# Two more kinds of traffic in the first FFN: ten pairs as seven block products, and weight blocks split ahead along another route

## The chip, the cores and the metric

The kernel runs on one core of a Trainium2 chip. The metric is device time in microseconds (us) of one execution, lower is better. The kernel before takes 1269.9 us, the median of 3 runs (1269.84 to 1270.08).

A core has engines that run side by side, each through its own queue of instructions in order: TensorE (PE in the profile, with PEld for the loads of its weights), VectorE (DVE), ScalarE (ACT), GpSimd (POOL) and SyncE (SP). SP, and here also POOL, issue transfers (DMAs); an instruction that waits holds up all that stands behind it in its own queue and nothing else, until somebody needs its result.

## The reference

Two layers over 512 tokens with 16 learned tokens in front (528 columns), width 1024. Each layer is a mixer and an FFN:

```
def mixer_sublayer(h, ...):
    u = rms_norm(h, pre_g);  z = u @ w_in       # q,k,v, forget logits, conv and short-conv inputs
    y = concat[ FoX attention (8 heads), Conformer conv module, short gated conv ]
    y = head_rms_norm(y) @ w_out
    return h + rms_norm(y, post_g)

def ffn_sublayer(h, pre_g, post_g, w_up, conv_w, w_down):
    u = rms_norm(h, pre_g)
    z = causal_depthwise_conv(u @ w_up, conv_w)  # w_up: 1024 x 5632, 3 taps
    g, up = jnp.split(z, 2, axis=-1)             # 2816 columns each
    y = (silu(g) * up) @ w_down                  # 2816 x 1024
    return h + rms_norm(y, post_g)
```

All inputs and outputs are float32.

## The kernel before, in words

**Splitting.** Every product is made in TensorE's fp32r form out of two rounded parts of each operand: `hi` is the rounded value, `lo` is what is left, and a product is the sum of hi·hi, hi·lo and lo·hi, three matmuls for each block of 128 rows of the contraction (`mm3`, L833, and `product`, L2281). Each weight block of 512 KB is therefore loaded raw by a DMA, rounded to `hi` by ACT ("CAST") and `lo` is made by DVE (raw minus hi). `prep_one` does this some blocks ahead of TensorE; the kernel calls the tiles `raw`, `whi`/`wlo`, `shi`/`slo`.

**The FFN.** The 2816 gate columns and the 2816 up columns make 22 *pairs* f of 128 gate and 128 up columns. They run in three parts, f = 0 to 7, 8 to 14 and 15 to 21; after each part come eight *down* products (one for each 128 output rows, over that part's pairs). A plain pair is 2 blocks x 8 row groups x 3 matmuls x 2 column halves = 96 matmuls of 264 columns. Between TensorE's products ACT evacuates them and DVE and ACT do the three-tap convolution, the gate, and the split of the result (`ffn_gate`; its rounded part is `ghi`, the rest `glo`).

**Seven block products.** A pair in the set `SEVEN[l]` is computed by `seven_pair` as a 2x2 block matrix product with seven instead of eight block products (Winograd's form of Strassen's method): 7 x 4 row groups x 3 = 84 matmuls of 264 columns. In place of the up block it needs sums of weight blocks: a block `c`, a summed block `b` (tiles `shi`, `slo`, one buffer each) and a half block `d` (a free `y` pair). The sums of the input columns are made once per layer (`t`).

**Where the weight sums come from.** They are made beforehand and kept in DRAM (`w_sum`), in one of two ways. `sum_steps` makes them by accumulating DMAs of GpSimd: three copies on SP and three accumulations on POOL for each pair; either spread over a mixer, whose order of work a planner with due times sets, or in the FFN, one step at each pair, started by a small copy on POOL ("tick", L2199). `down_sums` makes them with DVE during the down products: two loads, four additions and two stores for each pair. For this it uses four spare slices of the residual tile `h` (`spare_tile(0)` to `spare_tile(3)`, 1024 columns each). The residual is kept in DRAM from the end of the first part until the last seven pair (`h_dram`), so these slices are free in the second and third part; `raw_tile` also uses them for raw weight blocks, two of seven from slices 2 and 3.

**Blocks split ahead.** Six 512 KB blocks of the next layer's `w_in` are split in the first FFN and stored as hi and lo (`w_split`), so that the next mixer only has to load them. `store_one` runs at each pair of the second part (f = 8 to 14): it splits the block that the last call fetched, with tiles `shi`/`slo` of the seven pairs, and stores both parts on GpSimd's queue, then fetches the next one on SP into a raw tile.

**What sets the order.** In the FFN it is the order of the written loops, with a few constraints (`tc.issue_after`), which order two instructions of the same engine without a wait between engines. A scheduler fills the queues from there; a load waits for the last reader or writer of its target buffer.

## Time and profile before

| | |
|---|---|
| median of 3 runs | 1269.9 us (1269.84 to 1270.08) |
| profiled execution: own time, span | 1270.68 us, 1269.0 us |
| PE busy | 1249.8 us (98%), 9590 instructions |
| PEld busy | 1198.2 us (94%) |
| DVE busy | 920.9 us (73%) |
| ACT busy | 705.2 us (56%) |
| POOL busy | 162.0 us (13%) |
| first FFN: first gate convolution; first down product evacuated; first seven pair | at 285.1; 365.3; 524.2 us |
| second FFN: last product of a seven pair; last gate convolution | at 1205.4; 1217.3 us |

The span is the time from the first to the last instruction of the profiled execution; its own time as measured is 1.7 us more. A row of the *chain of waits* follows the work that ended last. A row of a *timeline* is one instruction: start, duration, engine, line, operation, output, input, and in brackets how long its engine sat idle before it and what ended that. A row of *windows* gives for each stretch (from:to, length) the busy time and number of instructions of PE, PEld, DVE, ACT and POOL, then the granted clock of TensorE, the busy share of the DMA engines and their rate in GB/s. SPq and POOLq are the queues from which SP and POOL issue transfers; "DMA to landing" is the time from an issue to the transfer's end.

### The profile page before, as it was taken

What the parts mean: (1) busy time and instruction counts of PE and PEld (TensorE: products, weight loads), DVE (VectorE), ACT (ScalarE), POOL (GpSimd) and SP (SyncE); (2) the same over time, 40 slices, a digit from 0 to 9 for tenths busy, and PEclk for the clock granted to TensorE, in tenths of its full rate; (3) what the DMA queues carried; (4) which work ended last, traced back from release to release, by engine and by line L of the source; (5) the groups of instructions that cost most, each with busy time, mean ns of one, the idle gap of its engine ahead of it and who ended that gap; (6) DMA issues with size and microseconds to landing.
All of it is one profiled execution on the core that took longest, in us unless ns stands there. A gap on an engine that the chain in (4) does not pass through costs nothing.

```text
span 1269.0 us, 24272 instructions
## 1 busy us (share of the span) xinstructions
PE 1249.8 (98%) x9590; PEld 1198.2 (94%) x9590; DVE 920.9 (73%) x1569; ACT 705.2 (56%) x1365; POOL 162.0 (13%) x343
## 2 busy tenths in 40 slices
PE   8999999999999999999999999999999999999997
PEld 8998898999999999999999988999999799979996
DVE  7887866589874665587688878656799748756954
ACT  7254576654444643476673545775554447526763
POOL 1324311001101100000003244110021000000000
PEclk9999999999999999999999999999999999999999
DMA  7257231726558634544552584547166655475611
GB/s 243 81 155 175 72 102 53 249 86 151 182 164 313 212 112 142 205 165 144 192 205 61 159 191 113 143 118 233 70 166 184 172 176 169 152 241 160 202 61 67
DMA packets 76146, 197.93 MB, mean 156 GB/s; under 512 B 8240, under 2 KB 18608, under 8 KB 75520
## 3 DMA queue, kind: packets, MB, share of 16 engines
q1 hardware_dynamic: 64048, 162.69, 40.0%
q0 software_dynamic: 11984, 33.69, 11.1%
q8 instruction: 75, 1.23, 0.4%
q14 instruction: 39, 0.32, 0.1%
HBM read 162.17 MB, written 44.30 MB: 163 GB/s over the span
## 4 chain that ended last, share of the span: by engine, by line
PE 66%; DVE 2%; ACT 1%; issue 0%; DMA 0%; POOL 0%; DVEq 0%; ACTq 0%
PE psum L833 45%; PE psum L2281 14%; PE psum L1403 2%; PE psum L1667 2%; PE psum L970 1%; PE psum L1633 1%; PE psum L1589 0%; DMA h<-w_sum 0%; DVE yp L1046 0%; PE psum L1733 0%; PE psum L1319 0%; DVE h L1056 0%; POOL dm L1604 0%; DVE ulo L1064 0%; DVE wlo L649 0%
## 5 line engine op out<-in xcount | busy, mean ns | idle before, releaser
L833 PE MATMUL psum<-y,whi 128*128 128x264 f32 (+3 forms) x1968 | 384.7, 299 | 2.7 <-ACT yp L2403 1.4
L833 PEld LDWEIGHTS psum<-y,whi 128*128 128x128 f32 x1968 | 305.1, 188 | 17.2 <-ACT yp L2403 2.6
L833 PE MATMUL psum<-uhi,whi 128*128 128x264 f32 (+1 forms) x1264 | 310.3, 288 | 1.6 <-ACT uhi L2065 0.8
L833 PE MATMUL psum<-ulo,whi 128*128 128x264 f32 (+1 forms) x1264 | 304.1, 284 | 0.6 <-DVE ulo L2067 0.4
L833 PE MATMUL psum<-uhi,wlo 128*128 128x264 f32 (+1 forms) x1264 | 303.2, 284 | 0.0
L833 PE MATMUL psum<-y,wlo 128*128 128x264 f32 (+3 forms) x984 | 273.9, 297 | 1.1 <-DVE wlo L789 1.1
L833 PEld LDWEIGHTS psum<-uhi,whi 128*128 128x128 f32 x1264 | 216.0, 188 | 5.9 <-issue 1.6
L833 PEld LDWEIGHTS psum<-ulo,whi 128*128 128x128 f32 x1264 | 216.1, 188 | 1.3 <-DVE ulo L2067 0.6
L833 PEld LDWEIGHTS psum<-uhi,wlo 128*128 128x128 f32 x1264 | 215.6, 188 | 0.0
L833 PEld LDWEIGHTS psum<-y,wlo 128*128 128x128 f32 x984 | 177.6, 188 | 6.7 <-DVE wlo L789 1.6
L2169 DVE SCALAR_TENSOR_TENSOR c<-zs,pv,c 128x528 f32<-128x528 f32 (+1 forms) x176 | 130.9, 757 | 18.4 <-ACT c L2167 16.4
L648 ACT CAST whi<-raw 128x1024 fp32r<-128x1024 f32 (+1 forms) x67 | 68.2, 1021 | 98.4 <-PE psum L833 72.6
L789 DVE TENSOR_TENSOR wlo<-raw,whi 128x1024 fp32r<-128x1024 f32 (+2 forms) x80 | 95.4, 1203 | 29.8 <-ACT whi L785 29.5
L649 DVE TENSOR_TENSOR wlo<-raw,whi 128x1024 fp32r<-128x1024 f32 (+1 forms) x67 | 79.4, 1185 | 28.1 <-ACT whi L648 28.0
L785 ACT CAST whi<-raw 128x1024 fp32r<-128x1024 f32 (+2 forms) x80 | 81.7, 1031 | 24.9 <-PE psum L833 18.0
L1149 DVE SCALAR_TENSOR_TENSOR cacc<-apad,pv,cacc 128x528 f32<-128x528 f32 x120 | 87.7, 772 | 0.1
L2167 ACT ACTIVATE c<-zs,pv 128x528 f32<-128x528 f32 (+1 forms) x88 | 63.1, 727 | 7.0 <-DVE zs L2132 2.7
L2281 PE MATMUL psum<-uhi,whi 128*128 128x258 f32 (+1 forms) x216 | 61.2, 284 | 0.0
L2281 PE MATMUL psum<-ulo,whi 128*128 128x258 f32 (+1 forms) x216 | 61.0, 283 | 0.0
L2281 PE MATMUL psum<-uhi,wlo 128*128 128x258 f32 (+1 forms) x216 | 60.5, 282 | 0.0
L2281 PE MATMUL psum<-t,shi 128*128 128x258 f32 (+1 forms) x288 | 54.2, 283 | 0.0
L1667 PE MATMUL psum<-pf,vals 128*128 128x400 f32 (+3 forms) x160 | 50.7, 399 | 0.6 <-POOL pf L1647 0.6
(273 smaller groups left out, 2193.2 us busy)
## 6 DMA issues: line engine op xcount, KB each, us to landing
raw<-in_w_dram SPq DMA_DIRECT2D x115, 512.0 KB, 4.5
h<-in_w_dram SPq DMA_DIRECT2D x27, 512.0 KB, 4.8
raw<-in_w_dram SPq DMA_DIRECT2D x30, 448.0 KB, 5.1
raw<-w_sum SPq DMA_DIRECT2D x18, 512.0 KB, 5.1
h<-w_sum SPq DMA_DIRECT2D x18, 512.0 KB, 5.4
h<-in_w_dram POOLq DMA_DIRECT2D x16, 512.0 KB, 3.8
w_sum<-h POOLq DMA_DIRECT2D x16, 512.0 KB, 5.3
w_sum<-in_w_dram SPq DMA_DIRECT2D x20, 256.0 KB, 5.0
```

Of the source, the lines that this page charges most:

```text
L648: nc.scalar.copy(hi[:, :sz], raw[:, :sz])
L649: last_low[0] = nc.vector.tensor_sub(lo[:, :sz], raw[:, :sz], hi[:, :sz].bitcast(F32))
L785: nc.scalar.copy(box["hi"][:, :sz], box["raw"][:, :sz])
L789: nc.vector.tensor_sub(lo[:, :sz], box["raw"][:, :sz], box["hi"][:, :sz].bitcast(F32))
L833: nc.tensor.matmul(d, lhsT=w[a][:, k, cols], rhs=rhs(b, k, hf), start=start and i == 0 and p == 0, stop=stop and i == n - 1 and p == 2)
L970: nc.tensor.matmul(ps, lhsT=om_d, rhs=box["c"][:, i, :], start=j + i == 0, stop=j + 1 == n_parts and i == tiles[-1])
L1149: nc.vector.scalar_tensor_tensor(conv[j], in0=src, in1=conv[j], scalar=col("a_dw_w", CK * j + i), op0=ALU.mult, op1=ALU.add)
L1403: nc.tensor.matmul(ps[:n, :nw], lhsT=(uhi, ulo)[ui][:, k, P * b:P * b + n], rhs=w[wi][:, k % 4, :], start=k == 0 and p == 0, stop=k == KD ...
L1667: nc.tensor.matmul(acc[:, s0 - qa:qz - qa], lhsT=vals[:, b].rearrange("p h d -> p (h d)")[:, o:o + P], rhs=box["p"], start=b == 0, stop=b ...
L2167: nc.scalar.activation(dst, src[:, 2:2 + 2 * fw], AF.Copy, scale=wtap(2, t))
L2169: nc.vector.scalar_tensor_tensor(dst, in0=src[:, i:i + 2 * fw], scalar=wtap(i, t), in1=dst, op0=ALU.mult, op1=ALU.add)
L2281: nc.tensor.matmul(psum[:, bank, :n7], lhsT=w[a][:, k0 + k, :], rhs=rhs(b, k), start=start and k == 0 and p == 0, stop=stop and k == K2 - ...
```

## The change

**More seven pairs in the first FFN.** Its set goes from six (15 to 20) to ten (10 to 13 and 15 to 20). The second FFN keeps its twelve. The table `SUMS` now says for each layer which pairs' sums are made where, in five places: in the FFN before, in the mixer, in the same FFN by accumulating DMAs, and in the first and the second down products:

| | FFN before | mixer | same FFN | first down | second down |
|---|---|---|---|---|---|
| layer 0, before | – | 15, 16 | – | 17, 18 | 19, 20 |
| layer 0, now | – | 10, 11, 12, 13 | 17, 18 | 15, 16 | 19, 20 |
| layer 1, before | 8, 9 | 10, 11, 12, 13 | 15, 16 | 17, 18 | 19, 20 |
| layer 1, now | 8, 9, 10 | 11, 12, 13 | 15, 16 | 17, 18 | 19, 20 |

**The summed block b behind c.** `split_next` loads and splits a block; for a summed block b it orders the load, the cast and the subtraction behind those of the block before it (which is c) on their engines. All else keeps a free order.

**Blocks split ahead.** `fetch_one` fetches a block on GpSimd's queue into spare slice 3 at f = 8, 10, 12, 15, 17, 19; `store_one` casts it into slice 2, subtracts in place in slice 3 and stores both on GpSimd's queue, at f = 10, 12, 14, 17, 19, 20, ordered behind the last gate's casts. As long as blocks are still to be fetched or stored, `raw_tile` leaves slices 2 and 3 alone.

```
-SEVEN = ((15, 16, 17, 18, 19, 20), (8, 9, 10, 11, 12, 13, 15, 16, 17, 18, 19, 20))
-SUMS = {0: (0, 2, 0), 1: (2, 4, 2)}
-DOWN_SUMS = 2
+SUMS = (((), (10, 11, 12, 13), (17, 18), (15, 16), (19, 20)),
+        ((8, 9, 10), (11, 12, 13), (15, 16), (17, 18), (19, 20)))
+FETCH, STORE = (8, 10, 12, 15, 17, 19), (10, 12, 14, 17, 19, 20)
+SEVEN = tuple(sorted(sum(places, ())) for places in SUMS)
...
+    def split_next(raw, src, hi, lo, sz, in_order=False):
+        with ExitStack() as order:
+            for last in (last_load, last_high, last_low) if in_order else ():
+                order.enter_context(tc.issue_after(last[0].ins))
+            last_load[0] = nc.sync.dma_start(raw, src)
+            flat = raw if raw.ndim == 2 else raw.rearrange("p e s -> p (e s)")
+            last_high[0] = nc.scalar.copy(hi[:, :sz], flat)
+            last_low[0] = nc.vector.tensor_sub(lo[:, :sz], flat, hi[:, :sz].bitcast(F32))
...
     def raw_tile():
         if spare[0] is not None and not in_spare[0]:
-            j = (None, 0, None, 1, None, 2, 3)[n_raw[0] % 7]
+            more = () if to_store or fetched else (2, 3)
+            j = (None, 0, None, 1, None, *more)[n_raw[0] % (5 + len(more))]
...
-    def store_one():
-        if fetched:
-            i, sz, raw = fetched.popleft()
-            hi, lo = (T(tx[0], [P, 2 * SB], F32R, t) for t in ("shi", "slo")) if sz <= 2 * SB else (T(wp, [P, CHUNK], F32R, t) for t in ("whi", "wlo"))
-            nc.scalar.copy(hi[:, :sz], raw[:, :sz])
-            nc.vector.tensor_sub(lo[:, :sz], raw[:, :sz], hi[:, :sz].bitcast(F32))
-            stored[i] = T(dram, [P, 2, sz], F32, f"w_split{i}")
-            for n, t in enumerate((hi, lo)):
-                nc.gpsimd.dma_start(stored[i][:, n], t[:, :sz].bitcast(F32))
-        if to_store:
-            i = to_store.popleft()
-            sz = chunks[i][3] * chunk_cols(chunks[i])
-            raw = raw_tile()
-            nc.sync.dma_start(raw[:, :sz], wflat[offs[i]:offs[i] + P * sz].rearrange("(p s) -> p s", p=P))
-            fetched.append((i, sz, raw))
+    def fetch_one():
+        i = to_store.popleft()
+        sz = chunks[i][3] * chunk_cols(chunks[i])
+        nc.gpsimd.dma_start(spare_tile(3)[:, :sz], wflat[offs[i]:offs[i] + P * sz].rearrange("(p s) -> p s", p=P))
+        fetched.append((i, sz))
+
+    def store_one(ghi_ins, glo_ins):
+        i, sz = fetched.popleft()
+        hi, lo = (spare_tile(j)[:, :sz] for j in (2, 3))
+        with tc.issue_after(ghi_ins[max(ghi_ins)].ins), tc.issue_after(glo_ins[0].ins):
+            nc.scalar.copy(hi.bitcast(F32R), lo)
+            nc.vector.tensor_sub(lo.bitcast(F32R), lo, hi)
+        stored[i] = T(dram, [P, 2, sz], F32, f"w_split{i}")
+        for n, t in enumerate((hi, lo)):
+            nc.gpsimd.dma_start(stored[i][:, n], t)
...
-                    if l == 0 and part == 1:
-                        store_one()
+                    if fetched and f in STORE:
+                        store_one(ghi_ins, glo_ins)
+                    if l == 0 and f in FETCH:
+                        fetch_one()
```

Below are three places in the order of instructions. A number after a name (`raw_6898`) tells apart the tiles that use the same buffers in turn; `h_2848` (`h_2834` before) is the spare part of the residual tile. The lines of the changed kernel are some five to ten off those of the kernel before: L646 became L570 (`split_next`), L648 became L572. In brackets stands what an instruction waits for: DMAHW is a transfer issued by SP, DMASW one issued by POOL, DVE or Activation an instruction of that engine.

**Place 1: SP at the end of the first FFN's last part**, before the change. The third row loads the up block of the plain pair 21 into a spare slice:

```order
L646 DMA raw_6846<-in_w_dram 128x1024 [waits DMAHW7_49,DVE_49]
L646 DMA raw_6940<-in_w_dram 128x896 [waits DMAHW5_49,DVE_49]
L646 DMA h_2834<-in_w_dram 128x1024 [waits DMAHW0_49,DVE_49]
L2350 DMA h_2834<-h_dram_112 128x1056 [waits DMAHW2_49,DVE_49]
L646 DMA raw_6996<-in_w_dram 128x896 [waits DMAHW4_49,DVE_49]
```

And now:

```order
L570 DMA raw_6898<-in_w_dram 128x1024 [waits DMAHW7_49,DVE_49]
L570 DMA raw_6992<-in_w_dram 128x896 [waits DMAHW0_49,DVE_49]
L570 DMA raw_7048<-in_w_dram 128x896 [waits DMAHW5_49,DVE_49]
L786 DMA raw_7128<-in_w_dram 128x896 [waits DMAHW4_49,DVE_49]
L570 DMA h_2848<-in_w_dram 128x1024 [waits DMAHW1_49,DMASW4_49,DVE_49]
L2357 DMA h_2848<-h_dram_112 128x1056 [waits DMAHW3_49]
L2357 DMA h_2848<-h_dram_112 128x1056 [waits DVE_49]
```

The same load stands two rows of down weights later, and it waits also for a transfer of POOL: it goes into spare slice 2, from which the sixth block's hi part is stored.

**Place 2: POOL and ACT at the last two blocks split ahead.** POOL now (L665 the fetch, L677 the two stores of a block, hi first; L2204 and L534 a tick and its accumulation):

```order
L677 DMA w_split_644_6696<-h_2848 128x1024 [waits Activation_49]
L677 DMA w_split_644_6696<-h_2848 128x1024 [waits DMASW1_49,DVE_49]
L665 DMA h_2848<-in_w_dram 128x1024 [waits DMASW2_49,DMASW1_49]
L2204 COPY cols_103<-y_653_6761 128x1 [waits Activation_49,Pool_49]
L534 DMA w_sum_10_392_3563<-w_sum_10_392_3563 128x512 [waits DMASW7_49,DMASW3_49]
L677 DMA w_split_659_6832<-h_2848 128x1024 [waits Activation_49]
L677 DMA w_split_659_6832<-h_2848 128x1024 [waits DMASW5_49,DVE_49]
```

ACT now, from the cast of the sixth block (L673) to the cast of pair 21's up block (`whi_6957`):

```order
L572 CAST shi_6836<-raw_6835 128x1024 [waits DMAHW4_49,PE_49]
L2326 COPY zs_2841<-psum_67 128x264 [waits PE_49]
L673 CAST h_2848<-h_2848 128x1024 [waits DMASW2_49,DMASW0_49]
L2184 ACTIVATE c_6885<-c_6885 128x528 [waits DVE_49]
L572 CAST y_663_6854<-h_2848 128x512 [waits DMAHW1_49,PE_49]
L2332 COPY zs_2841<-psum_67 128x264
L2172 ACTIVATE c_6889<-zs_2841,pv_3_69 128x528 [waits DVE_49,Activation_49]
L2320 COPY zs_2841<-psum_67 128x264 [waits PE_49]
L2172 ACTIVATE c_6979<-zs_2841,pv_3_69 128x528 [waits DVE_49]
L2373 COPY zs_2841<-psum_67 128x264 [waits PE_49] x2
L2188 CAST y_667_6895<-c_6885 128x528 [waits DVE_49,Pool_49]
L572 CAST whi_6957<-h_2848 128x1024 [waits DMAHW1_49]
```

None of the L665, L673 and L677 rows was there before; the sixth cast waits for the sixth fetch, and the sixth fetch for the fifth store out of slice 3.

**Place 3: ACT in the first down products of the second FFN**, before the change (`shi` is a summed block b, the L2403 copies evacuate down products):

```order
L2226 CAST uhi_108<-yp_10196 128x2x514
L2238 CAST t_1061_11069<-acc_11851 128x516 [waits DVE_49]
L638 CAST shi_12036<-h_10200 128x1024 [waits DMAHW1_49,DMASW1_49]
L2238 CAST t_1063_11071<-acc_11855 128x516 [waits DVE_49]
L648 CAST whi_11906<-raw_11904 128x1024 [waits DMAHW7_49,PE_49]
L2403 COPY yp_10196<-psum_67 128x512 [waits PE_49]
```

And now:

```order
L572 CAST whi_11986<-raw_11985 128x1024 [waits DMAHW6_49,PE_49]
L2410 COPY yp_10241<-psum_67 128x512 [waits DVE_49,PE_49]
L572 CAST whi_12016<-h_10245 128x1024 [waits DMAHW1_49,PE_49]
L2410 COPY yp_10241<-psum_67 128x512 [waits PE_49]
L572 CAST whi_12047<-raw_12046 128x1024 [waits DMAHW7_49,DVE_49,PE_49]
L572 CAST shi_12080<-h_10245 128x1024 [waits DMAHW0_49,DMASW3_49]
L2410 COPY yp_10241<-psum_67 128x512 [waits DVE_49,PE_49]
```

The same cast of the summed block now stands four evacuations later, right behind the cast of its pair's block c.

18 lines of the change are left out of this document (5 added, 13 removed).

## The prediction, as it stood before the changed kernel was run

> **What bounds the kernel now.** I read the page's busy times first, then the chain of waits, then windows of the stretches that the change touches, then single rows around the waits.
>
> ```profile
> span 1269.0 us, 24272 instructions
> PE 1249.8 (98%) x9590; PEld 1198.2 (94%) x9590; DVE 920.9 (73%) x1569; ACT 705.2 (56%) x1365; POOL 162.0 (13%) x343
> ```
>
> TensorE is busy for 98% of the span, so time can only be saved by giving it less to do or lost by making it wait. The chain has long rows of one line without a break, and they give the price of a matmul:
>
> ```profile
> 365.99 126.71 PE psum L833 x1038
> 524.32 49.77 PE psum L2281 x410
> ```
>
> 49.77 us / 410 = 0.1214 us for one 264-column matmul of a seven pair, 126.71 / 1038 = 0.1221 in plain pairs. The windows say how near the other engines are. A row has the stretch, then PE, PEld, DVE, ACT, POOL; the first is one seven pair, the next two are the mixers of layer 0 and layer 1:
>
> ```profile
> 554.50:564.60 10.10, 10.10 (x86) 10.10 (x85) 8.75 (x11) 7.85 (x15) 0.00 (x0) 1.00 0.51 164
> 73.10:209.50 136.40, 134.54 (x982) 122.26 (x982) 102.85 (x249) 84.02 (x219) 39.18 (x87) 1.00 0.44 115
> 704.90:841.30 136.40, 134.58 (x986) 122.61 (x985) 105.05 (x252) 83.86 (x219) 43.76 (x91) 1.00 0.59 144
> ```
>
> In a seven pair DVE works 8.75 of 10.10 us and ACT 7.85, yet TensorE is full: it holds, with little to spare. The granted clock is 1.00 in all rows.
>
> **The change, part by part.**
>
> *Fewer matmuls.* Pairs 10 to 13 go from 96 to 84 matmuls: 4 x 12 = 48, and the order of the changed kernel has just 48 fewer on TensorE. At 0.1214 us that is **-5.8 us** (-5.9 by the plain price).
>
> *DVE and ACT in the new seven pairs.* They get the load of the row 554.50. On top come the splits for storing, three in seven pairs' time, each one cast and one subtraction as in the first two rows (a group's busy time, then the mean ns of one):
>
> ```profile
> L648 ACT CAST whi<-h 128x1024 fp32r<-128x1024 f32 x2 | 2.1, 1051 | 0.7 <-PE psum L2281 0.5
> L649 DVE TENSOR_TENSOR wlo<-h,whi 128x1024 fp32r<-128x1024 f32 x2 | 2.4, 1216 | 0.0
> L2169 DVE SCALAR_TENSOR_TENSOR c<-zs,pv,c 128x528 f32<-128x528 f32 x15 | 11.5, 766 | 1.2 <-ACT c L2167 1.1
> ```
>
> 8.75 + 1.22 = 9.97 of 10.1 us on DVE, 7.85 + 1.05 = 8.9 on ACT. It fits into one pair by 0.1 us, and the next pair, without a store, has 1.35 us free. What hides it is the weight blocks split ahead of TensorE. I take 0; if a store's subtraction found no block ahead it would cost its own 1.22 us once, so at worst 3 x 1.2 = 3.6 us for the three stores of the second part.
>
> *Four sums in a mixer instead of two (layer 0), three instead of four (layer 1).* The two mixers of the kernel before are the test: with two sums and with four, both take 136.40 us with 134.54 and 134.58 us of PE. The two extra sums move 4.58 us more onto POOL and cost nothing. I take 0, between -0.3 and +0.3. The ticks' sums use only POOL (13% busy) and free stretches of the queues: 0.
>
> *b behind c.* Timeline of ACT in the second FFN's first down products:
>
> ```profile
> 1010.22 1.05 ACT L638 CAST shi<-h 128x1024 fp32r<-128x1024 f32 x1 [5.33 <-DMA h<-w_sum]
> 1011.17 0.62 ACT L2238 CAST t<-acc 128x516 fp32r<-128x516 f32 x1
> 1011.69 1.05 ACT L648 CAST whi<-raw 128x1024 fp32r<-128x1024 f32 x1
> 1012.64 0.58 ACT L2403 COPY yp<-psum 128x512 f32<-128x512 f32 x1
> ```
>
> and TensorE just behind:
>
> ```profile
> 1012.35 0.61 PE L833 MATMUL psum<-y,whi 128*128 128x512 f32 x2
> 1012.80 0.40 PE L833 MATMUL psum<-y,wlo 128*128 128x512 f32 x1
> 1013.27 0.73 PE L833 MATMUL psum<-y,whi 128*128 128x512 f32 x2
> ```
>
> ACT stood 5.33 us for the load of a summed block, with a weight cast and an evacuation queued behind; TensorE's matmul at 1013.27 came 0.47 us after the one before, where the two of 1012.35 took 0.45 together, 0.23 each. In the changed order this cast stands four evacuations later (place 3). The gain is what TensorE lost: 0.24, taken as **-0.3 us**, between 0 and -0.5. Later itself, this b is not late: it is first needed in the seven pairs behind the down products, whose run on the chain starts 20 us on:
>
> ```profile
> 1030.53 49.26 PE psum L2281 x408
> ```
>
> *Fetch and store on GpSimd's queue.* For the first five blocks two pairs' time (some 20 us) lies between fetch and store, against landings of under 8 us. The last is fetched at f = 19 and stored at f = 20, and behind it hangs something that TensorE needs. Durations of such transfers (issue to landing; shi and slo are the stores of now):
>
> ```profile
> h<-in_w_dram SPq DMA_DIRECT2D x27, 512.0 KB, 4.8
> h<-in_w_dram POOLq DMA_DIRECT2D x16, 512.0 KB, 3.8
> w_split<-shi POOLq DMA_DIRECT2D x6, 512.0 KB, 3.9
> w_split<-slo POOLq DMA_DIRECT2D x6, 512.0 KB, 6.7
> ```
>
> One block's two stores on POOL before, hi and lo:
>
> ```profile
> 426.99 0.53 POOL L666 DMA_DIRECT2D w_split<-shi  x1 [9.28 <-ACT shi L662]
> 428.25 0.53 POOL L666 DMA_DIRECT2D w_split<-slo  x1 [0.73 <-DVE slo L663]
> ```
>
> The lo store goes 1.26 us behind the hi store and lands 6.7 - 3.9 + 1.26 = 4.1 after it: the two share a queue. Next, ACT's casts of the last two seven pairs:
>
> ```profile
> 568.55 1.05 ACT L638 CAST shi<-h 128x1024 fp32r<-128x1024 f32 x1 [1.30 <-PE psum L2281]
> 578.99 1.05 ACT L638 CAST shi<-raw 128x1024 fp32r<-128x1024 f32 x1 [1.41 <-PE psum L2281]
> 580.76 1.04 ACT L648 CAST whi<-h 128x1024 fp32r<-128x1024 f32 x1
> ```
>
> The first two are the casts of pair 19's and 20's block b, each let go when TensorE is through with the b before; the third is that of pair 21's up block, loaded here in good time:
>
> ```profile
> 570.88 0.33 SPq L646 DMA_DIRECT2D h<-in_w_dram  x1
> ```
>
> Call the moment at which pair 18's b comes free, 568.5 on this clock, zero. In the changed order the fifth cast for storing stands right ahead of pair 19's b cast, so at 0.7 (behind ACT's queue), done at 1.7; its subtraction (1.22) ends at 2.9 with nothing in front on DVE and at 3.7 with one multiply-add (0.77, the L2169 row); I take 3.5. The store out of slice 3 goes at 3.5 and lands 6.7 later, 10.2. The sixth fetch, into slice 3, waits for that: +3.8 = 14.0. The sixth cast would have come at 11.7, behind pair 20's b cast (579.0 to 580.0) and a copy, and is held until 14.0; with 1.05 its store out of slice 2 goes at 15.1 and lands 3.9 later, 19.0. Pair 21's up block now loads into slice 2 (place 1: its row waits for a POOL transfer): +4.8 = 23.8, cast 1.05 = 24.9, subtraction 1.22 = 26.1. In the changed order TensorE has 168 matmuls from zero to the first that reads this block: 168 x 0.1214 = 20.4. So it waits 4.5 us for the hi part, does six matmuls (0.7), and waits 0.5 for lo: **+5.0 us**. The bounds come from the shortest and the longest landing of the nearest lines (the stores' line, GpSimd's loads in the down products, the raw loads):
>
> ```profile
> L666 POOL DMA_DIRECT2D w_split<-slo x6: 533/533/536, 381.5 to 439.5; - x6
> DMA to landing us min/median/max: 3.2/5.9/7.1
> L590 POOL DMA_DIRECT2D h<-in_w_dram x8: 530/535/587, 314.2 to 1087.6; - x8
> DMA to landing us min/median/max: 3.4/4.2/7.0
> L646 SPq DMA_DIRECT2D h<-in_w_dram x25: 327/328/382, 377.5 to 1188.5; - x25
> DMA to landing us min/median/max: 3.1/4.6/7.4
> ```
>
> With the shortest (3.2, 3.4, 3.2, 3.1) the fetch lands at 10.1, the cast isn't held, the store goes at 12.8 and lands at 16.0, the load at 19.1, and the cast is done at 20.2: TensorE waits at most 0.5 for lo. With the longest (7.1, 7.0, 7.1, 7.4) the load lands at 10.6 + 7.0 + 1.1 + 7.1 + 7.4 = 33.2 and the stall is 14.4. Behind the waiting load on SP stand the residual's reloads and down weights that are due later; behind the waiting cast on ACT the first casts of the last down products, which then come together with it. I take nothing more for these. While the sixth cast is held, ACT's copies behind it are 2.3 us late, less than a pair ahead.
>
> *The fifth store ahead of pair 19's b cast.* A cast of 1.05 at 0.7 moves that b cast to 1.75, done at 2.8; TensorE needs it after 24 matmuls, 2.9; the lo part, behind DVE's added subtraction, comes about 0.3 late: **+0.3**, between 0 and +1.
>
> The sum: 1269.0 - 5.8 - 0.3 + 5.0 + 0.3 = 1268.2 of span. The profiled execution took 1270.68, 1.7 more than its span, and is 0.8 above the median of the runs shown: 1268.2 + 1.7 - 0.8 = **1269.1 us**, no change that a measurement of this kernel can tell (0.2%, 2.5 us).
>
> **The rivals.**
>
> *A, the forecast: the up block is late, and gives back more than half of what is saved.* The stall lies between 3.3 and 8.3 us, so that the time stays within 2.5 us of 1269.9: 1267.4 to 1272.4. For it: the changed order has each of the four waits, and each transfer has its median in a row. Against it: it stands on four medians in a row.
>
> *B, the transfers are short, and the saving stays.* If the lo store, now 1.8 us behind hi instead of 1.26, needs only 4.1 from its own issue, it lands at 7.6, the fetch at 11.4, so the sixth cast runs at its own 11.7; then 12.8 + 3.9 + 4.8 = 21.5, cast 22.6: the stall is 2.2 + 0.5 = 2.7, the time 1269.1 - 2.3 = 1266.8. With the shortest landings the stall is 0.5: 1264.6. Against it: before, in the same second part, lo's median is 6.7 with the same neighbour in the queue, and SP moves 164 GB/s beside it. The Trainium skill ("DMA: Bandwidth & Descriptors", Anatomy of one DMA — SWDGE (gpsimd) path) fits a GpSimd-issued transfer as 2.0 us plus its bytes over 436 GB/s; the estimate from this page for 512 KB is 3.2 us, by which three of the four transfers would be at their shortest and the time B's lower end. The rows here, 3.8, 3.9 and 6.7, are all longer, so I give it less than A.
>
> *C, slower: the same chain of slice 3, slice 2 and the up block at its longest.* Lo and fetch at their longest, 3.5 + 7.1 + 7.0 = 17.6, cast to 18.7, the hi store at its line's median 5.9, the load 4.8: 29.4, cast 30.5, a stall of 10.1 + 0.5 = 10.6 and a time of 1269.1 + 5.6 = 1274.7; with all four at the longest 1278.5. It decides from a stall of 8.3 us on. For it speaks that the ticks' accumulations stand between the stores on GpSimd's queue (the L534 row of place 2) and wait for transfers of their own.
>
> *D, the new pairs starve.* DVE at 9.97 of 10.1 us finds no block ahead and the three stores cost their 3.6 us, on top of A: 1272.7. Against it the full TensorE of the row 554.50, with the same work on DVE but for the store.
>
> *E, the change does not do what it says*: out, since the order has the 48 matmuls fewer.
>
> **How the numbers follow.** A 0.50, B 0.34, C 0.12, D 0.04. A is within 0.2% of 1269.9; B is faster by more; C and D are slower by more: faster 0.34, same 0.50, slower 0.16. The time is A's, 1269.1. The range takes in most of B, whose lowest is about 1264, and A's upper end: 1264.2 to 1272.6; it leaves out C and the edges, some 0.2. Cases of both signs stand beside A; its own range is given there.
>
> **What the changed profile would show.** TensorE with 48 matmuls fewer, at 0.1214. A stall of PE right behind pair 20's b products, before the first product of pair 21's up block, put down to the cast `whi` of a spare slice, with ACT having waited for a load into `h`, and before it the third store of slice 2 landing about 3.9 after the sixth cast. The sixth cast held for the fetch: ACT idle, put down to a transfer `h<-in_w_dram`. No stall in pairs 10 to 13 and no longer mixer in layer 0; 0.3 us less around the second FFN's first down products. Wrong would be: no stall at pair 21 (B), a stall over 8 us (C), or gaps of TensorE spread over pairs 10 to 14 (D).

## The result: 1.2% slower, and the profile after

| | before | after |
|---|---|---|
| median | 1269.99 us (1269.84 to 1270.39, 4 runs) | 1285.03 us (1283.16 to 1286.01, 4 runs) |
| ratio | | 1.0116 (95% interval 1.0099 to 1.0134) |
| profiled execution: time, span | 1270.68, 1269.0 us | 1285.44, 1283.7 us |

The forecast was 1269.1 us, between 1264.2 and 1272.6. The changed kernel is 15 us slower, beyond the dearest case of the prediction (1278.5). Of the runs below, one execution of e_none_ring5 (1724.8 us, granted clock 0.65) and one of e_early_split (4298.3 us) fell in a slow state, and no number rests on them.

Page of the changed kernel: span, busy times, and the granted clock in 40 slices.

```profile
span 1283.7 us, 24294 instructions
PE 1251.1 (97%) x9542; PEld 1198.2 (93%) x9542; DVE 930.6 (72%) x1585; ACT 712.1 (55%) x1381; POOL 183.5 (14%) x373
PEclk9999999999999989998999999999999999999999
```

TensorE has 48 instructions fewer, as counted, but is busy 1.3 us longer, and the granted clock has two slices below 9, where every slice was at 9 before (mean clock 0.994 against 1.000).

Where the time went is read by setting the start of each ACT and DVE instruction against the same instruction of the kernel before. The difference is constant over long stretches and moves at few places; each row is what it moves by in a stretch (the stretches by the clock of the kernel before):

| stretch | forecast | measured |
|---|---|---|
| first mixer (90 to 215) | 0 | +1.5 |
| first FFN, first part (to 365) | 0 | 0.0 |
| second part, pairs 8 to 14 (to 516) | -5.8 | +1.9 |
| last part, pairs 15 to 21 (to 604) | +5.3 | +12.3 |
| second mixer (to 870) | 0 | +0.1 |
| second FFN | -0.3 | -0.4 |

The rest to the 14.7 us between the spans, -0.7, lies at the two ends. So 7.7 us were lost in the second part on top of the 5.8 that were saved there, and 12.3 in the last. Four rows of what TensorE waited for in the changed kernel (total, times, longest):

```profile
PE psum L2286 <- ACT acc L2316: 5.7, 1, 5.7
PE psum L838 <- ACT whi L572: 5.0, 2, 2.5
PE psum L2286 <- ACT whi L572: 1.5, 2, 1.1
PE psum L1594 <- issue: 1.4, 1, 1.4
```

None of these stood on that list before; of the shorter waits only one is new, 0.5 us for a lo part (L573) in the last part. The first row is one wait in the second part, the next two lie in the last part, and the fourth, at 110 us, is the first mixer's 1.5. The profile names nothing that this fourth one waited for, and its cause stays open.

**The second part.** ACT's timeline around the 5.7 us:

```profile
447.73 0.37 ACT L2326 COPY zs<-psum 128x264 f32<-128x264 f32 x1
454.92 1.04 ACT L673 CAST h<-h 128x1024 fp32r<-128x1024 f32 x1 [6.82 <-DMA h<-in_w_dram]
456.14 0.38 ACT L2316 COPY acc<-psum 128x264 f32<-128x264 f32 x1
```

The cast of a block split ahead stands in ACT's queue 6.82 us for its fetch; the copy that TensorE needs stands behind it. It is the second of the six, stored at f = 12, since its store below is the second on POOL's queue (the expectations below call it the third, at f = 14, by mistake). The fetch (L665) and the stores that it had to wait for (L677), on POOL:

```profile
433.58 1.11 POOL L677 DMA_DIRECT2D w_split<-h  x2
444.56 0.56 POOL L665 DMA_DIRECT2D h<-in_w_dram  x1 [2.46 <-DMA w_split<-h]
456.26 0.55 POOL L677 DMA_DIRECT2D w_split<-h  x1 [2.71 <-ACT zs L2322]
```

The times to landing of all fetches and all stores, by their two lines:

```profile
L665 POOL DMA_DIRECT2D h<-in_w_dram x6: 532/532/555, 385.9 to 587.4; - x6
DMA to landing us min/median/max: 3.5/5.4/10.3
L677 POOL DMA_DIRECT2D w_split<-h x12: 531/552/1036, 433.6 to 593.6; - x12
DMA to landing us min/median/max: 4.7/7.4/9.9
```

The stores issued at 433.6 landed by 444 and the fetch issued at 444.56 at 454.9, 10.3 us later: 21 us for a lo store and a fetch that the prediction's rows put at 6.7 + 3.8. The windows show what went with it: in the ten us before the stall the transfer engines were full (share 1.01, the last number but one). Before:

```profile
435.00:445.00 10.00, 10.00 (x84) 10.00 (x84) 6.43 (x8) 6.82 (x11) 1.07 (x2) 1.00 0.64 210
445.00:455.00 10.00, 10.00 (x85) 10.00 (x84) 5.85 (x8) 4.90 (x9) 0.00 (x0) 1.00 0.36 122
```

After:

```profile
435.00:445.00 10.00, 10.00 (x84) 10.00 (x83) 7.47 (x11) 6.70 (x14) 1.29 (x2) 1.00 1.01 287
445.00:455.00 10.00, 5.86 (x49) 5.65 (x47) 4.63 (x7) 2.27 (x5) 1.34 (x3) 0.94 0.99 280
```

**The clock.** Windows of 2 us from that stall on, and behind two stalls of the last part:

```profile
450.00:452.00 2.00, 0.86 (x8) 0.65 (x6) 0.00 (x0) 0.00 (x0) 0.00 (x0) 1.00 1.00 312
452.00:454.00 2.00, 0.00 (x0) 0.00 (x0) 0.00 (x0) 0.00 (x0) 0.84 (x1) 0.93 1.03 409
454.00:456.00 2.00, 0.00 (x0) 0.00 (x0) 0.01 (x1) 1.08 (x2) 0.00 (x0) 0.50 1.06 326
456.00:458.00 2.00, 1.42 (x6) 1.43 (x7) 1.22 (x1) 2.00 (x5) 1.04 (x2) 0.50 0.81 231
458.00:460.00 2.00, 2.00 (x11) 2.00 (x10) 1.97 (x2) 1.74 (x4) 0.05 (x1) 0.50 0.96 374
460.00:462.00 2.00, 2.00 (x17) 2.00 (x16) 1.26 (x3) 0.67 (x2) 0.00 (x0) 0.86 0.93 268
590.00:592.00 2.00, 2.00 (x12) 2.00 (x11) 2.00 (x3) 1.08 (x3) 0.33 (x1) 0.57 0.73 205
592.00:594.00 2.00, 2.00 (x12) 2.00 (x11) 1.28 (x2) 0.58 (x2) 0.96 (x2) 0.58 1.19 231
604.00:606.00 2.00, 1.91 (x9) 1.91 (x9) 2.00 (x3) 1.71 (x4) 0.00 (x0) 0.50 0.93 302
606.00:608.00 2.00, 2.00 (x14) 2.00 (x13) 0.80 (x2) 0.00 (x0) 0.00 (x0) 0.67 0.84 302
```

Behind each of the three longest stalls TensorE runs at half its clock, with 9 to 12 matmuls in 2 us instead of 18 or 19. This lasts 4.0 us behind the first stall, having begun within it, and 3.4 us behind each of the others (the missing clock of the rows, 0.43 x 2 + 0.42 x 2 = 1.7 us, is 3.4 us at half). Busy time times the missing clock: 1.42 x 0.5 + 2 x 0.5 + 2 x 0.14 = 2.0 us behind the first, 2 x 0.43 + 2 x 0.42 = 1.7 and 1.91 x 0.5 + 2 x 0.33 = 1.6 behind the others, 5.3 in all. The Trainium skill ("TensorE: Matmul & The Clock Gate", Part 1) says that the array's clock is halved after an idle window of about 3.4 us and comes back after a busy one. The first stall, 5.7 us, is longer than this, but the clock fell already 2.9 us into it (TensorE stops at 450.9, and the 0.93 of the second row puts the fall at 453.7). The two waits of 2.5 us are shorter than that window and had the same effect, so here the measurement decides and not the rule.

**The last part.** ACT's casts that waited for loads there:

```profile
572.88 1.04 ACT L572 CAST whi<-h 128x1024 fp32r<-128x1024 f32 x1 [1.85 <-DMA h<-in_w_dram]
586.98 1.04 ACT L572 CAST whi<-raw 128x1024 fp32r<-128x1024 f32 x1 [3.56 <-DMA raw<-in_w_dram]
590.99 1.05 ACT L673 CAST h<-h 128x1024 fp32r<-128x1024 f32 x1 [0.92 <-DMA h<-in_w_dram]
602.15 1.04 ACT L572 CAST whi<-h 128x1024 fp32r<-128x1024 f32 x1 [1.66 <-DMA h<-in_w_dram]
```

The fourth is the forecast's wait, pair 21's up block in slice 2, and the third the sixth cast held by its fetch; both are there and shorter than forecast. The first two were not forecast: plain weight loads of SP that came late. TensorE's waits in this part (5.0 + 1.5 + 0.5 us) and the 3.3 us of clock make 10.3 of the 12.3 us; the other 2.0 are not accounted for.

### The profile page after: what moved, and what is told of

The parts are those of the page before. It is cut to its first block, busy times and chain, and to the rows that moved or that the text cites. A ratio compares the mean times of both kernels' runs of the same rounds, so it can differ in the third digit from the quotient of the medians.

```text
span 1283.7 us, 24294 instructions
## 1 busy us (share of the span) xinstructions
PE 1251.1 (97%) x9542; PEld 1198.2 (93%) x9542; DVE 930.6 (72%) x1585; ACT 712.1 (55%) x1381; POOL 183.5 (14%) x373
## 5 line engine op out<-in xcount | busy, mean ns | idle before, releaser
L838 PE MATMUL psum<-uhi,whi 128*128 128x264 f32 (+1 forms) x1136 | 286.1, 290 | 6.5 <-ACT whi L572 5.0
L838 PE MATMUL psum<-ulo,whi 128*128 128x264 f32 (+1 forms) x1136 | 279.2, 285 | 0.6 <-DVE ulo L2072 0.4
L838 PE MATMUL psum<-uhi,wlo 128*128 128x264 f32 (+1 forms) x1136 | 278.6, 285 | 0.5 <-DVE wlo L573 0.5
L838 PEld LDWEIGHTS psum<-uhi,whi 128*128 128x128 f32 x1136 | 197.4, 190 | 11.3 <-ACT whi L572 5.4
L838 PEld LDWEIGHTS psum<-ulo,whi 128*128 128x128 f32 x1136 | 197.2, 189 | 1.3 <-DVE ulo L2072 0.6
L838 PEld LDWEIGHTS psum<-uhi,wlo 128*128 128x128 f32 x1136 | 197.0, 190 | 0.7 <-DVE wlo L573 0.7
L572 ACT CAST whi<-raw 128x1024 fp32r<-128x1024 f32 (+1 forms) x80 | 81.8, 1026 | 121.5 <-PE psum L838 90.1
L573 DVE TENSOR_TENSOR wlo<-raw,whi 128x1024 fp32r<-128x1024 f32 (+1 forms) x80 | 95.2, 1191 | 41.0 <-ACT whi L572 40.4
L2286 PE MATMUL psum<-uhi,whi 128*128 128x258 f32 (+1 forms) x264 | 75.7, 287 | 6.8 <-ACT acc L2316 5.7
L2286 PE MATMUL psum<-uhi,wlo 128*128 128x258 f32 (+1 forms) x264 | 75.0, 285 | 0.0
L2204 POOL COPY cols<-y 128x1 f32<-128x1 f32 x28 | 20.3, 726 | 340.7 <-ACT y L2188 340.5
```

Source lines behind the costliest of these rows:

```text
L572: last_high[0] = nc.scalar.copy(hi[:, :sz], flat)
L573: last_low[0] = nc.vector.tensor_sub(lo[:, :sz], flat, hi[:, :sz].bitcast(F32))
L838: nc.tensor.matmul(d, lhsT=w[a][:, k, cols], rhs=rhs(b, k, hf), start=start and i == 0 and p == 0, stop=stop and i == n - 1 and p == 2)
L2204: t = nc.gpsimd.tensor_copy(ticks, src.bitcast(F32))
L2286: nc.tensor.matmul(psum[:, bank, :n7], lhsT=w[a][:, k0 + k, :], rhs=rhs(b, k), start=start and k == 0 and p == 0, stop=stop and k == K2 - ...
```

## The experiments

Three theories. **1, crowded transfers**: the four more seven pairs and the ticks' accumulations fill the transfer engines. **2, the chain through one slice**: fetch, cast and store wait for each other, and ACT and POOL pass the wait on. **3, the raw ring**: with slices 2 and 3 taken, the weight loads have five raw buffers instead of seven, are issued later, and come late.

A table of all of them first, by the same reckoning as above (what the offset to the kernel before moves by in a stretch of the profiled execution, one for each kernel; "second part" includes the -5.8 of ten seven pairs where there are ten):

| kernel | seven pairs | split ahead | raw buffers | first mixer | first part | second part | last part | second mixer | ratio to before (95%) |
|---|---|---|---|---|---|---|---|---|---|
| the changed kernel | 10 | slices, f = 8 to 20 | 5 | +1.5 | 0.0 | +1.9 | +12.3 | +0.1 | 1.0116 (1.0099 to 1.0134) |
| e_order_only | 6 | old way | 7 | -0.6 | 0.0 | 0.0 | 0.0 | +0.5 | 1.0002 (0.9993 to 1.0011) |
| e_old_sums | 6 | slices | 5 | -0.1 | 0.0 | 0.0 | +10.1 | -0.3 | 1.0077 (1.0062 to 1.0093) |
| e_old_store | 10 | old way | 7 | -0.1 | 0.0 | +30.3 | 0.0 | -0.2 | 1.0237 (1.0223 to 1.0251) |
| e_free | 10 | slices | 5 | +0.4 | 0.0 | +2.0 | +11.5 | 0.0 | one run, 1284.24 us |
| e_none | 10 | none | 7 | -0.1 | 0.0 | -5.9 | 0.0 | +5.6 | 0.9997 (0.9986 to 1.0008) |
| e_two | 10 | slices | 5 | +0.8 | 0.0 | +0.6 | +9.5 | +0.3 | 1.0078 (1.0055 to 1.0100) |
| e_ring5 | 6 | old way | 5 | +0.1 | 0.0 | 0.0 | +4.0 | +0.2 | 1.0034 (1.0023 to 1.0046) |
| e_fourblocks | 10 | slices, four blocks | 5 | +1.3 | 0.0 | +0.4 | +15.3 | +3.1 | 1.0150 (1.0131 to 1.0168) |
| e_none_ring5b | 10 | none | 5 | +0.8 | 0.0 | +0.2 | +6.1 | +4.2 | 1.0113 (1.0096 to 1.0131) |
| e_early_raw | 10 | old way, f = 3 to 9 | 7 | +0.5 | +2.3 | -5.9 | 0.0 | -0.4 | 0.9987 (0.9976 to 0.9998) |
| e_pool | 10 | the same, lo by GpSimd | 7 | +0.8 | +9.2 | -5.9 | 0.0 | -0.3 | 1.0028 (1.0017 to 1.0040) |
| e_down | 10 | old way, down products | 7 | +1.3 | +3.6 | -4.5 | 0.0 | +0.6 | 1.0001 (0.9992 to 1.0010) |
| e_early_late | 10 | old way, f = 3 to 9, ticks from f = 8 | 7 | -0.1 | +0.5 | -0.3 | 0.0 | +0.6 | 0.9982 (0.9972 to 0.9992) |
| e_early_split | 10 | old way, f = 3 to 9, ticks f = 1, 2 and from 10 | 7 | -0.1 | +3.9 | -5.7 | -0.2 | +0.6 | 1.0003 (0.9993 to 1.0012) |

The second FFN moves by 0.0 to -0.4 in all of them. Executions of one kernel differ by several us (e_none: 1268.3 to 1272.2), so the small entries carry little.

### The order of b alone, and without it

e_order_only is the kernel before with `split_next` alone; e_free is the changed kernel without the order:

```
-            split_next(..., src, hi, lo, sz, kind == "b")
+            split_next(..., src, hi, lo, sz)
```

> The kernel before with one part of the change: block b ordered behind c, the old six seven pairs, the old sums and the old way of splitting ahead. In the changed kernel the time against the kernel before falls by 0.32 us at the first and 0.08 us at the second down products of the second FFN, and nowhere else could the order be seen by itself. If that is the order's doing: 0.4 us faster than before, 1269.5. If the order also binds something in the first FFN's last part (where the changed kernel lost 12.3 us), it is slower than before by some of these.

> The changed kernel with block b in free order again. If the order only brings the 0.4 us of the second FFN: 1285.4. If it also makes loads or casts wait in the first FFN's last part, where SyncE's queue stood behind c's load more than once: 1278 to 1283, with smaller stalls of TensorE after 572 us.

Measured: 1270.33 us against 1270.14 (11 and 15 runs), no difference; and 1284.24, with the losses of the changed kernel. The -0.3 us in the second FFN comes in e_free too, which has no order, and in kernels with the old order it comes or not. One of these, e_ring5 (below), shows what it is. ACT waits as before for the summed block, a little shorter (4.87 us instead of 5.33):

```profile
1014.94 1.05 ACT L638 CAST shi<-h 128x1024 fp32r<-128x1024 f32 x1 [4.87 <-DMA h<-w_sum]
1016.42 1.05 ACT L648 CAST whi<-raw 128x1024 fp32r<-128x1024 f32 x1
```

and TensorE does not miss a beat there (0.23 us from matmul to matmul); the offset falls by 0.4 to 0.5 us at this place too, after having risen by as much earlier in this FFN:

```profile
1017.30 0.40 PE L833 MATMUL psum<-y,wlo 128*128 128x512 f32 x1
1017.53 0.61 PE L833 MATMUL psum<-y,whi 128*128 128x512 f32 x2
1017.99 0.40 PE L833 MATMUL psum<-y,wlo 128*128 128x512 f32 x1
```

So the 0.24 us that the prediction saw lost there belong to one execution, not to the order. The order is worth nothing that these runs show.

### The two halves of the change apart

e_old_sums has the old sets and places of the sums with the new way of splitting ahead:

```
+SUMS = (((), (15, 16), (), (17, 18), (19, 20)),
+        ((8, 9), (10, 11, 12, 13), (15, 16), (17, 18), (19, 20)))
```

e_old_store has the new sets with the `store_one` and the seven raw buffers of the kernel before.

> The changed kernel with the old sets and the old places of the sums: six seven pairs in the first FFN, no accumulations by ticks after f = 9; the new order and the new way of splitting ahead stay. Theory 1 (crowded transfers: the four more seven pairs' loads and the ticks' accumulations fill the DMA engines, and the store chain through slice 3 is late because of them): no stall of the third cast at f = 14, no loss in the first mixer, and the last part at most 3 us; time 1269.5 to 1273. Theory 2 (the chain of store, fetch and cast through one slice is too long by itself): the third cast still holds ACT and TensorE by 3 to 6 us in the second part; 1275 or more. Theory 3 (five raw buffers instead of seven make the loads of the last part late): the second part is whole, but the last part still loses 8 to 12 us: 1278 to 1282.

> The changed kernel with the old way of splitting ahead (fetch by SyncE into a raw tile, stored at each f of the second part through the seven pairs' own tiles, seven raw buffers): ten seven pairs, the new sums and the new order stay. Theory 1 (crowded transfers): TensorE still stalls in the second part by several us, since the same bytes move in a shorter time: 1270 to 1280. Theories 2 and 3 (the slice chain and the raw ring): both parts are free of these stalls; what is left is -5.8 for the matmuls, -0.4 for the order and +1.4 in the first mixer: 1265.2.

Measured: 1280.25 and 1300.10 us, the second far outside both of its expectations. With six seven pairs the second part loses nothing, with the same chain through slice 3; its transfers are light there:

```profile
435.00:445.00 10.00, 10.00 (x84) 10.00 (x83) 6.18 (x7) 5.49 (x10) 0.53 (x1) 1.00 0.46 163
445.00:455.00 10.00, 10.00 (x84) 10.00 (x83) 5.87 (x7) 5.53 (x9) 0.53 (x1) 1.00 0.27 92
```

The last part, however, loses 10.1 of the 12.3 us with the old sets: this belongs to the new way of splitting ahead. And with the old way the last part loses nothing, though ten seven pairs, ticks and sums are there. Beside seven pairs in the second part, however, the old way loses 36 us there. It uses the one `shi`/`slo` tile that the seven pairs use, and ACT's queue stands for its loads; that this is the whole cause is argued, since the seven pairs' traffic is there too:

```profile
POOL w_split L670 <- ACT shi L666: 13.7, 2, 7.5
ACT shi L666 <- DMA h<-in_w_dram: 11.4, 2, 7.4
```

So neither theory alone: the second part needs ten seven pairs and the slices, the last part needs the slices only.

### No blocks split ahead; the ticks early; five raw buffers in the kernel before

e_none has `MASK` all zero. It leaves no work out: the second mixer splits the six blocks itself. e_two:

```
-                        todo.popleft()()
+                        for _ in range(min(2, len(todo))):
+                            todo.popleft()()
```

e_ring5 is the kernel before with this (`seven_raw` is set at f = 20):

```
-            j = (None, 0, None, 1, None, 2, 3)[n_raw[0] % 7]
+            j = (None, 0, None, 1, None, 2, 3)[n_raw[0] % (7 if seven_raw[0] else 5)]
```

> The changed kernel without any block split ahead: nothing is fetched or stored in the first FFN, seven raw buffers all along, and the second mixer splits the six blocks itself. Theory 1 (crowded transfers: seven pairs 10 to 13 and the ticks fill the DMA engines by themselves): TensorE still stalls by several us in the second part. Theory 2 (the chain through one slice is the cause, and the others only stretch it): no stall of more than 1 us in the first FFN, its second part 5.8 us shorter than before, its last part as before. The second mixer gets some us longer, by what splitting ahead is worth.

> The changed kernel with two steps of the sums at each tick instead of one, so that the twenty steps are done by f = 10 and no accumulation runs beside the seven pairs 10 to 13. If the ticks' transfers are what stretched the third block's fetch from 4 to 10.3 us: no stall in the second part, which is then 5.8 us shorter than before, and the last part loses 10, as with the old sums: 1274 to 1275. If the seven pairs' own loads do it: still 4 to 8 us of stall and half clock in the second part, 1281 to 1286.

> The kernel before with one thing taken from the change: five raw buffers instead of seven in the first FFN until f = 20 (slices 2 and 3 are left alone, and nobody uses them). Theory 3 (the missing buffers make the last part's loads late): most of the 10.1 us that the changed kernel with the old sums lost in the last part: 1276 to 1280. Theory 2 (the casts, stores and fetches through slices 2 and 3 themselves): 0 to 1 us, 1270 to 1271.

Measured: 1269.76, 1279.72 and 1274.77 us. Without splitting ahead the ten seven pairs bring their whole saving, -5.9 us in the second part, and no load makes TensorE wait in the first FFN. What it waits for from 365 to 620:

```profile
PE psum L838 <- ACT yp L2410: 0.5, 1, 0.5
PE psum L838 <- DVE yp L2412: 0.3, 1, 0.3
```

And this although the transfer engines are just as full as in the changed kernel:

```profile
435.00:445.00 10.00, 10.00 (x85) 10.00 (x84) 7.21 (x11) 6.85 (x14) 0.94 (x2) 1.00 1.03 310
445.00:455.00 10.00, 10.00 (x85) 10.00 (x85) 8.32 (x13) 7.52 (x14) 1.43 (x2) 1.00 0.93 284
```

The crowd is made by the seven pairs' loads and the ticks, without any store (theory 1), but it costs nothing by itself: the blocks fetched ahead cover it. The saving is then given back in the second mixer, which takes 5.6 us longer: that is what splitting six blocks ahead is worth, in this execution with half the clock behind a wait of 2.3 us (DVE's `zs`, L990). In e_none_ring5b, below, the same wait of 2.3 us has no slower clock behind it, and the mixer takes 4.2 us longer. With two steps at each tick (e_two) the last accumulation is issued at 437, and the second part is still 6.4 us above the -5.8 instead of 7.7. So the accumulations behind 437 are worth little; two of them still fall into the crowded stretch, so that the share of the ticks in it is not settled. And e_ring5 is 4.0 us slower in the last part with nothing but two raw buffers fewer. The 10.1 us of e_old_sums had come out as theory 3 expected, but the ring by itself makes less than half of them.

### The ring by itself beside ten seven pairs, and two blocks left out

e_none_ring5 is e_none with five raw buffers until f = 20. e_none_ring5b is the same kernel once more, and the numbers are from there; the other execution of e_none_ring5 took 1285.79 us. e_fourblocks:

```
-FETCH, STORE = (8, 10, 12, 15, 17, 19), (10, 12, 14, 17, 19, 20)
+FETCH, STORE = (8, 10, 15, 17), (10, 14, 17, 19)
-MASK = "111111..."
+MASK = "111100..."
```

> The changed kernel with four blocks split ahead instead of six: fetched at f = 8, 10, 15, 17 and stored at f = 10, 14, 17, 19; the second mixer splits the other two itself. The fetch ahead of the store at f = 14 has four pairs' time instead of two, and no block follows the one stored at f = 19, so that seven raw buffers are used from there on. Theory 2 (the wait of the third and the sixth cast on fetches through one slice): no stall in the second part, which is 5.8 us shorter than before, and the last part loses less than the 12.3 of the changed kernel by its sixth block's share, the forecast's 5 us or more. Theory 1 (crowding by what else moves): the second part still loses 2 us or more. The second mixer pays up to 5.7 x 2 / 6 = 1.9 us; time 1270 to 1274 by theory 2, 1277 or more by theory 1.

> The changed kernel without any block split ahead, but still with five raw buffers until f = 20 in the first FFN, as if slices 2 and 3 were in use; the second mixer splits the six blocks itself. With seven buffers and no stores the first FFN had no stall at all. If the missing buffers alone make the last part's loss of 10 to 12 us: the same here. If they are worth the 4.0 us that they cost the kernel before, and the rest is the casts, stores and fetches: 3 to 5 us between 520 and 620, and in the second part, where the seven pairs' loads and the ticks fill the transfer engines, 0 to 3 us.

> The same kernel as the one without blocks split ahead and with five raw buffers, once more, since its profiled execution was disturbed; its one undisturbed time was 1285.8, 16 us above the same kernel with seven buffers. If the missing buffers make the last part's loss by themselves: 10 us or more of offset between 520 and 620, as in the changed kernel (12.3). If they act where seven pairs' loads and ticks fill the transfers: most of the 16 in the second part, and 4 in the last.

Measured: 1288.99 us for e_fourblocks and 1284.51 for e_none_ring5b, 14.8 above e_none with two buffers fewer. Its second part is 6.0 us above the -5.8, its last part +6.1; these two are what the buffers can be charged with. Nothing is split ahead in it, so no cast, store or fetch can be meant; ACT waits for a plain weight load:

```profile
451.69 1.04 ACT L572 CAST whi<-raw 128x1024 fp32r<-128x1024 f32 x1 [5.69 <-DMA raw<-in_w_dram]
```

It was issued 9 us before. The load of e_none in the same ordinal place of SP's weight loads, the second of the two in its row, went out by 434.4, more than 8 us earlier. First e_none_ring5b, then e_none:

```profile
442.68 0.33 SPq L570 DMA_DIRECT2D raw<-in_w_dram  x1
```

```profile
432.65 1.80 SPq L570 DMA_DIRECT2D h<-in_w_dram  x2
```

This is the very place where the changed kernel waits for its second block, with the engines nearly as full:

```profile
435.00:445.00 10.00, 10.00 (x85) 10.00 (x84) 6.98 (x10) 6.57 (x13) 0.88 (x1) 1.00 0.94 216
445.00:455.00 10.00, 6.17 (x49) 5.74 (x48) 4.66 (x7) 4.31 (x8) 1.18 (x2) 1.00 0.80 228
```

e_fourblocks says the same from the other side: its second block is stored two pairs later and its wait is gone, and the second part loses 6.2 us all the same, on a raw load that ACT waits 6.3 us for. So theory 3 holds for the second part, with theory 1 as its condition: with six seven pairs the same five buffers cost nothing there (e_ring5, 0.0), and with ten the load goes out 8 us later and takes 9.0 us, which makes 6.0 of the 7.7 us. A full share alone does not set the landing: in e_none, at 1.03, the load issued at 432.65 took 7.0 us. The cast for storing is only the first to stand in front when it is there.

In the last part the ring alone costs 4.0 us with six seven pairs and 6.1 with ten. The casts, stores and fetches through the slices add 10.1 - 4.0 = 6.1 and 12.3 - 6.1 = 6.2. Which of them is **not settled**: without the sixth block (e_fourblocks) the last part should have been shorter and was longer, 15.3, with late loads up to the last down products. That kernel also goes back to seven raw buffers one pair earlier, which shifts which buffer is next; this was not tried apart.

### A place where six blocks can be split ahead

The slices are what the ring lacks, and the old way needs `shi`/`slo`, which are free before the first seven pair. e_early_raw is e_old_store with

```
-                    if l == 0 and part == 1:
+                    if l == 0 and 3 <= f <= 9:
                         store_one()
```

e_pool is that with the lo parts by `nc.gpsimd.tensor_sub`; e_down calls `store_one` at seven of the first part's down products instead; e_early_late has the ticks of the first FFN only from f = 8 on and two steps at each tick; e_early_split has four ticks at each of f = 1 and 2 and one from f = 10 on.

> The changed kernel with the old way of splitting ahead, but at f = 3 to 9, before the first seven pair, so that its tiles and transfers do not meet seven pairs: ten seven pairs, the new sums and the new order stay, seven raw buffers from f = 8 on. If what was lost is the meeting of stores and seven pairs: the second and the last part are free of stalls, -5.8 for the matmuls and -0.3 for the order, and the first part pays for DVE (69 of 80 us busy before, and 7 more here) with 0 to 3 us: 1264 to 1267. If the seven pairs and ticks alone crowd the transfers: 1268 or more, with stalls in the second part.

> The kernel that split ahead at f = 3 to 9 in the old way, with the lo parts of these six blocks made by GpSimd instead of DVE. There the first part cost 2.3 us, with DVE busy for 9.5 of 10 us around the stalls. If DVE's load was the reason: these 2.3 us go, 1266. If GpSimd's subtraction is so slow that the tiles come free late, or disturbs DVE: 1268 or more.

> The changed kernel with the old way of splitting ahead, one step at each of the first part's down products (after which DVE was busy for 3 to 4 of 10 us in the kernel before); ten seven pairs, the new sums and the new order stay. If the loss comes only from splitting ahead beside the seven pairs: no stall in the first FFN but those of before, -5.9 for the matmuls and -0.4 for the order: 1263.9. If two sums by DVE and six stores together are too much for the transfers there (0.9 busy from 375 to 395 before): 1266 or more, with stalls between 367 and 420.

> The kernel that split ahead at f = 3 to 9 in the old way, with the sums' ticks of the first FFN from f = 8 on, two steps each, so that their transfers no longer meet the stores in the first part (0.94 to 0.99 of the transfer engines' time there, against 0.55 before). If these transfers were the reason for the 2.3 us that the first part lost: -5.9 and -0.4 stay, 1264 to 1265.5. If it was DVE (9.5 of 10 us): 1266 to 1268 as with the ticks from the start. If the ticks then fill the second part's transfers: stalls there, 1268 or more.

> The kernel that split ahead at f = 3 to 9 in the old way, with the ticks of the first FFN kept away from these stores: four at each of f = 1 and 2, one at each of f = 10 to 21. With the ticks from f = 8 on, two steps each, the first part's loss fell from 2.3 to 0.5 us, but a weight load came late in the second part (4.1 us and half the clock behind it). If both losses are crowded transfers: 0.5 in the first part, none in the second, 1264.3. If the second part's late load comes by chance with any ticks beside seven pairs: times from 1264 to 1270, median near 1266.5.

Measured: 1267.97, 1273.67, 1270.57, 1266.98 and 1270.32 us. In e_early_raw the second part has its -5.9 and the last part no loss; the first part pays 2.3 us, where transfers and DVE are both full. 20 us of it, before and then e_early_raw:

```profile
340.00:360.00 20.00, 20.00 (x166) 20.00 (x165) 17.73 (x25) 9.53 (x13) 2.21 (x4) 1.00 0.55 138
```

```profile
340.00:360.00 20.00, 19.02 (x156) 18.84 (x155) 17.70 (x26) 11.72 (x18) 4.36 (x7) 1.00 0.94 291
```

DVE is no busier there than before; the transfers are. Moving the subtractions to GpSimd made it worse (9.2; 2.4 to 2.9 us each there, against 1.2 on DVE), moving the ticks away made it better (0.5 in e_early_late, where DVE is even busier from 285 to 365: 73.0 us against 71.6 in e_early_raw). So here too it is rather the transfers than DVE, but this is argued: TensorE's waits are put down to DVE (`zs`, L2136; 1.0 us here), and e_early_split, which also keeps ticks away from the stores, pays 3.9, after eight steps of sums at f = 1 and 2, with 3.0 us of such waits and outside what was expected of it. That part depends on more than was varied. e_down gives 3.7 us of its saving back in one wait of TensorE for ACT at the first down products. e_early_late is the fastest version found, 0.9982 (0.9972 to 0.9992). Most of its twelve runs lie near 1266.5 us; four lie between 1269.9 and 1272.9, and the profiled one is of these: a load came late beside the ticks,

```profile
468.41 0.94 ACT L572 CAST whi<-h 128x896 fp32r<-128x896 f32 x1 [7.79 <-DMA h<-in_w_dram]
```

and the second part lost 5.5 us, a stall of 3.8 and half clock. So it is near the same edge, and on one side of it by chance.

## Why the prediction was wrong

- **Fewer matmuls, -5.8 us**: right. e_none and e_early_raw have -5.9 in the second part.
- **DVE and ACT in the new seven pairs, 0**: right. In those two kernels the pairs 10 to 13 run without a stall; and in the changed kernel, where the stores' subtractions come on top, no wait of TensorE in the second part is put down to such a subtraction. So case D is out.
- **Four sums in a mixer, 0 with a bound of 0.3**: the bound was too narrow. The twelve kernels with the new sums lie between -0.1 and +1.5 there, the three with the old sums between -0.6 and +0.1. The same code gives both ends, so a single pair of windows, as the prediction had, could not show it; what makes the wait stays open. The windows also hid it: they compare stretches of equal length, in which a stall shows as less work.
- **b behind c, -0.3**: wrong. The 0.24 us were chance (e_ring5).
- **Fetch and store on GpSimd's queue**: this step failed, in three ways. (a) The diff's `raw_tile`, five buffers instead of seven, was read, told in the part on the change, and given no price. It is the largest one: by itself it costs 6.0 us of the 7.7 lost in the second part, and 4.0 to 6.1 of the 12.3 in the last. (b) "two pairs' time (some 20 us) lies between fetch and store, against landings of under 8 us": landings were taken from the kernel before, in which the engines were at 0.64 and 0.36 of their time at this place. At 1.0 a store took 9.9 and a fetch 10.3, and ACT was free for the second cast at 448.1, 17 us after the first (431.3), not 20. The traffic of four more seven pairs (two blocks and a half, c, b and d, in place of each up block) was counted nowhere. (c) The chain that was worked out, up to pair 21's up block, is there in all its steps, with other sizes: the lo store 8.7 instead of 6.7 us, the fetch 3.5 instead of 3.8, the hi store 6.0 instead of 3.9, and TensorE waits 2.4 us instead of 5.0. It was late itself: counted from the fifth cast (575.31), the block's hi part is ready after 27.9 us instead of 24.2, and TensorE gets to it after 25.5 instead of 19.7, behind the waits of 2.5 and 0.5 us at 588 and their slower clock.
- **A stall as long as the wait**: each of the three longest stalls also brought half the clock behind it, 5.3 us in all, which was in no term and no bound.
- The bounds of the stall, 0.5 to 14.4 us, were worked out for one place. Case C, slower by this one chain at its longest (1274.7 to 1278.5), had the right sign for the wrong reason: the chain was near the forecast's size, and the loss came from two places that it does not name.

## What to carry to other kernels

A buffer taken from a ring of prefetch tiles is a cost like an instruction: ask how late each load may then be issued, and how long it takes where the transfer engines are full, not on average. Count the bytes that a change adds per unit of the busiest engine's time in the stretch where they fall; a landing time from a light stretch is no bound for a full one. And price a stall of a few us with the slower clock behind it.

## What the runs showed of the hardware

- With the transfer engines' share near 1.0, 512 KB stores and fetches issued by GpSimd from 433 to 445 us took 9.1 to 10.3 us, against 3.5 at the least in the same kernel. In e_none, with a share of 1.03 and no stall, the loads had gone out early enough.
- In the changed kernel stalls of 2.5 us were followed by 3.4 us at a granted clock of 0.50, and the stall of 5.7 us by 4.0. The length of a stall alone does not decide: half the clock followed stalls of 1.5 and 1.6 us too (e_free at 600, e_two at 597), and none followed 2.1 us in e_early_split (at 337). The same wait of 2.3 us in the second mixer had it behind it in e_none and not in e_none_ring5b.
- The six subtractions of 128x1024 by GpSimd instead of DVE cost the first part 9.2 us instead of 2.3.
